# The RWKV-7 scan of a two-layer trunk: five chain outputs kept in PSUM until one copy, one operand for the states of both directions, and long VectorE instructions issued as two halves

## The chip, the cores and the metric

The kernel runs on one core of one Trainium2 chip. The metric is the device time of one execution in microseconds (us). Times of several runs are given by their median. Engines are called by their short names: PE (TensorE matmuls), PEld (the weight loads of PE), DVE (VectorE), ACT (ScalarE), POOL (GpSimd), SP (the queue that issues all DMAs here).

## What is computed

One inference step of a trunk of two layers, for 128 context tokens and 512 latent tokens of width 2048, all in float32. Layer 0 (attention) is not touched by the change. Layer 1 is a bidirectional RWKV-7 mixer with 32 heads of 64; its recurrence, cut to what matters, is:

```python
def wkv7_scan(s0, r, decay, k, v, kk, a, reverse):
    def step(s, inp):
        r_t, w_t, k_t, v_t, kk_t, a_t = inp
        sa = jnp.einsum('bhij,bhj->bhi', s, -kk_t)
        s = s * w_t[:, :, None, :] + sa[..., None] * (kk_t * a_t)[:, :, None, :] + v_t[..., None] * k_t[:, :, None, :]
        return s, jnp.einsum('bhij,bhj->bhi', s, r_t)
...
for z in range(2):                     # two directions, summed
    s_fin, y = wkv7_scan(s_init[z], r, decay[:, :, z], k_z, v, kk, a_z, z == 1)
    ...                                # group norm of y, bonus
y = (outs[0] + outs[1]) * silu(gate)
return y @ w_out
```

Context scans start from zero, latent scans from a given state of their direction; the final context states are outputs too.

## The kernel before, in words

Projections (`project_steps`, L111 to L128) multiply float32 numbers as three products of rounded parts: a weight tile arrives by DMA as `raw`, ACT rounds it to `whi` (L100), POOL subtracts to `wlo` (L101), and PE runs the products into the PSUM tile `pj` (L126), two halves of 320 tokens each. Such a pair of matmuls is the filler of the whole second layer: `fill(w)` (L1482) issues w pairs (`quota[1]` is 1 in the chain) between two pieces of other work.

The tokens (512 latent, 128 context) are ten chunks of 64. The scan goes by channel tile i (16 tiles of 128 channels, two heads each) and u (0 or 1, the two halves of the token axis as the two directions meet them), so 32 units (i, u). `unit(n)` (L1495) writes out PE's order by hand (`manual_schedule`, L1559). It has two parts. In part one the generator `stage_c` (L1284), the chain, advances through five chunk steps s = 0 to 4, and between its yields `P1` steps other stages (the inverse's preparation `stage_a3`, the rates `stage_a1` and group norm `stage_gn` of neighbouring units) and `fill` puts pairs of matmuls (`CW`, 3, 3, 2 and 3 by the yield's number). In part two the list `P2` interleaves the block inverse `stage_inv`, `stage_bk`, `stage_pre`, `stage_bonus` and the Gram products `stage_a2` of the next units with filler. The order on DVE, ACT, POOL and SP is not written by hand: a scheduler places each instruction by priority; `stage_c` and `stage_inv` are wrapped in `urgent` (L1470), which raises theirs. Every engine then works its own list strictly in order.

One chain step does this. PE multiplies the state S by a chunk's operand into C (L1330), DVE makes `rhs` from C and MV (L1337), PE multiplies it by the block inverse `xd` into `pu` (L1349), the two directions' halves of `pu` are copied to UV, one by ACT (L1351) and one by DVE (L1352), PE makes the state's increment `pn` (L1359) and the chunk's output part from UV (L1295, `y_uv`), DVE adds the old state (L1364 or L1374) and multiplies by the decay `dcj` (L1365 or L1376), and that is S of the next step. The output part from the old state is added on PE in the next step (L1303, `y_state`, ahead of L1330), and ACT then copies the output from `Y` to `Yn` (L1307, `y_out`).

All of C, Y, pu, pn and the scratch of the block inverse (PA, PB) lie in one PSUM tile `CC` of two banks. Where two engines touch the same bank, the framework makes the later instruction wait for the earlier one, also where both only read: L1307 waits for L1337, and L1349 waits for L1307.

A direction's state starts fresh (from `state`) or ends inside a tile, so in some steps only one direction has one: in u = 0 direction 1 begins at s = 2, in u = 1 direction 0 ends after s = 2. Then S is a list with None, the matmuls of the missing direction are left out, `rhs` is made for 64 rows by L1337 and for 64 by L1341, and the state is updated per direction (L1374 and L1376) instead of jointly (L1364 and L1365).

On DVE, beside the chain: the recursion of the inverse of 16 by 16 blocks (L1149 to L1166; its input `Lp` comes by DMA, its result goes by DMA to `Xd` and back to `DD`, which L1174 transposes), the k normalisation (L1029), the cumulated rates (L1075, a scan along tokens), operands (L1085 to L1099), the masks of the Gram products (L1120), the bonus (L1429), and the end of a tile (L1438, L1440).

Of the kernel before, what the change touches and what calls it, by code (L numbers as in the profile page):

```python
# [53 lines left out]
def kernel(  # L54
# [785 lines left out]
    with ExitStack() as l1:  # L840
# [24 lines left out]
        for t in xds + [Lpw]:  # L865
            dve.memset(t, 0.0)
# [10 lines left out]
        blkr = b1.tile([128, 128], F32R, name="blkr")  # L877
        act.activation(out=blkr, in_=blkm, func=AF.Copy)
# [141 lines left out]
        def stage_kk(i):  # L1020
# [8 lines left out]
            dve.scalar_tensor_tensor(out=kk, in0=t.kT, scalar=V("k_k", i), in1=kk, op0=ALU.mult, op1=ALU.mult)  # L1029
# [40 lines left out]
        def stage_e(i, u):  # L1070
# [4 lines left out]
            dve.tensor_tensor_scan(out=D, data0=scm, data1=rate, initial=0.0, op0=ALU.mult, op1=ALU.add)  # L1075
# [19 lines left out]
            dve.tensor_scalar(out=az, in0=az, scalar1=V("k_a", i), scalar2=ck1[:, i:i + 1], op0=ALU.mult, op1=ALU.add)  # L1095
# [29 lines left out]
        def stage_a3(i, u):  # L1125
# [35 lines left out]
            dve.tensor_tensor(out=sb[P_], in0=bc8(Xp[P_, lo8, lo8].rearrange("p s j -> p j s"), 1),
                              in1=bc8(Lp[P_, lo8, hi8].rearrange("p s r -> p r s"), 2), op=ALU.mult)
            dve.tensor_reduce(out=W[P_], in_=sb[P_], axis=AX.X, op=ALU.add)
            dve.tensor_tensor(out=sb[P_], in0=bc8(Xp[P_, hi8, hi8], 2),
                              in1=bc8(W[P_].rearrange("p q j -> p j q"), 1), op=ALU.mult)
            dve.tensor_reduce(out=Xp[P_, hi8, lo8], in_=sb[P_], axis=AX.X, op=ALU.add, negate=True)  # L1166
# [117 lines left out]
        def stage_c(i, u):  # L1284
            t, un = tiles_[i], units[(i, u)]
            AR, BKn, UV, xd, GG, dcj = un.AR, un.BKn, un.UV, un.xd, un.GG, un.dcj
            S, joint = carry.get("S"), carry.get("joint")
            Yn = un.Yn = u1.tile([128, 5, 2, 64], F32, tag="yz", name="Yn", bufs=2)
            Y = CC[:, :, 64:128]

            def y_uv(s, S, cgs):
# [5 lines left out]

            def y_state(s, S, cgs):
                for h in range(2):
                    hs = slice(64 * h, 64 * h + 64)  # L1300
                    for z in range(2):
                        if S[z] is not None:
                            pe.matmul(Y[64 * z:64 * z + 64, h, :], AR[hs, cgs[z], 1, :], S[z][hs, :],  # L1303
                                      start=False, stop=True)

            def y_out(s, S, cgs):
                act.activation(out=Yn[:, s], in_=Y, func=AF.Copy)  # L1307

            for s in range(5):
                loc = (s, 4 - s)  # L1310
                cgs = (un.ca[0] + loc[0], un.ca[1] + loc[1])
                if u == 0 and s == 0:
                    st = u1.tile([128, 64], F32, tag="st", name="st", bufs=2)
                    dma(out=st, in_=state[0, i])
                    S, joint = [st, None], None
                if u == 0 and s == 2:
                    st = u1.tile([128, 64], F32, tag="st", name="st", bufs=2)
                    dma(out=st, in_=state[1, i])
                    S, joint = [S[0], st], None
                if u == 1 and s == 3:  # L1320
                    S, joint = [None, S[1]], None
                C = CC[:, :, 0:64]
                pu, pn = (CC[:, 1, 128:256], CC[:, 0, 128:256]), CC[:, 0, 128:256]
                if s:
                    y_state(*ys)
                for h in range(2):
                    hs = slice(64 * h, 64 * h + 64)
                    for z in range(2):
                        if S[z] is not None:
                            pe.matmul(C[64 * z:64 * z + 64, h, :], AR[hs, cgs[z], 0, :], S[z][hs, :],  # L1330
                                      start=True, stop=True)
                rhs = u1.tile([128, 128], F32, tag="rhs", name="rhs")
                mv = un.MV[:, s, :]
                for p, ok in (((0, 128), True),) if None not in S else (((0, 64), S[0]), ((64, 128), S[1])):
                    p = slice(*p)
                    if ok is not None:
                        dve.scalar_tensor_tensor(out=rhs[p].rearrange("p (h d) -> p h d", h=2), in0=C[p],  # L1337
                                                 scalar=-1.0, in1=mv[p].rearrange("p (h d) -> p h d", h=2),
                                                 op0=ALU.mult, op1=ALU.subtract)
                    else:  # L1340
                        dve.tensor_scalar(out=rhs[p], in0=mv[p], scalar1=-1.0, scalar2=None, op0=ALU.mult)  # L1341
                if s:
                    y_out(*ys)
# [8 lines left out]
                dve.tensor_copy(out=UV[64:128, cgs[1], :], in_=pu[1][64:128])  # L1352
# [10 lines left out]
                if joint is not None and all(need):  # L1363
                    dve.tensor_tensor(out=Sn, in0=pn[:, 0:128].rearrange("p (z d) -> p z d", z=2), in1=joint, op=ALU.add)  # L1364
                    dve.tensor_tensor(out=Sn, in0=Sn,  # L1365
                                      in1=dcj[:, s, :].rearrange("p (z o) -> p z o", o=1).to_broadcast([128, 2, 64]),
                                      op=ALU.mult)
                else:
                    for z in range(2):
                        if not need[z]:  # L1370
                            continue
                        pz = pn[:, 64 * z:64 * z + 64]
                        if S[z] is not None:
                            dve.tensor_tensor(out=Sn[:, z, :], in0=pz, in1=S[z], op=ALU.add)  # L1374
                            pz = Sn[:, z, :]
                        dve.tensor_scalar(out=Sn[:, z, :], in0=pz, scalar1=dcj[:, s, z:z + 1], scalar2=None, op0=ALU.mult)  # L1376
# [57 lines left out]
        def stage_end(i, u):  # L1434
# [3 lines left out]
            dve.tensor_scalar(out=t.ysum, in0=t.ysum, scalar1=V("ln_w", i), scalar2=lnb2[:, i:i + 1],  # L1438
# [258 lines left out]
```

## Time and profile before

| What | Value |
|---|---|
| median of 3 runs | 3674.24 us (3662.57, 3674.24, 3682.79) |
| the profiled execution's own time | 3666.42 us |
| its span (first to last instruction) | 3664.6 us |
| mean granted clock of PE | 0.982 |
| busy in the span: PE, DVE, ACT, POOL | 94%, 60%, 44%, 33% |

The profile is of one execution. "Idle before" is the time in which an engine had nothing running ahead of an instruction, and the arrow names what released it. In a timeline row stand start, duration, engine, line, operation, output and inputs, count of merged instructions, and in brackets the idle time and its releaser. Matmuls are pipelined and their ends are modelled, so the idle time of PE is counted from a modelled end; that of PEld is counted from the last weight load, and comes out longer for the same gap.

### The profile page before, as it was taken

The numbers are of one execution on the slowest core, as the hardware profiler recorded it, in microseconds if no ns is written. First come the engines' busy times: TensorE is split into PE (matmuls) and PEld (weight loads), VectorE is DVE, ScalarE is ACT, GpSimd is POOL, SyncE is SP. The second block draws the span as 40 slices with busy tenths as digits, with TensorE's granted clock in tenths as the row PEclk, the third lists the DMA queues.
The fourth block names the chain that finished last, engine by engine and source line by source line (L and its number), as shares of the span: only waits on it lengthen the run. The fifth ranks groups of instructions, "written<-read, shape, count | busy, mean of one in ns | idle before, by whom it ended". The sixth has DMA issues, their size and how long they took to land. (4 is left out here: it accounts for less than half of the span.)

```text
span 3664.6 us, 83198 instructions
## 1 busy us (share of the span) xinstructions
PE 3443.2 (94%) x34176; PEld 3014.7 (82%) x34176; DVE 2190.1 (60%) x4232; ACT 1608.0 (44%) x3310; POOL 1192.0 (33%) x1094
## 2 busy tenths in 40 slices
PE   8999999999999999999999999999999999998998
PEld 4788889988888889888777777778888878777898
DVE  3346655666666674556666666766666666666402
ACT  3344443444444422544454454545454545545322
POOL 1222122222222344432332333323333333333444
PEclk9999999999999999999999999999999999999999
DMA  9623423333333464332222222222222222223534
GB/s 332 221 69 103 125 89 116 108 107 106 108 107 112 149 211 153 105 79 65 68 64 71 59 66 75 65 67 64 65 74 68 62 66 70 67 74 95 159 97 144
DMA packets 388462, 376.18 MB, mean 103 GB/s; under 512 B 200496, under 2 KB 242416, under 8 KB 388080
## 3 DMA queue, kind: packets, MB, share of 16 engines
q1 hardware_dynamic: 388080, 370.86, 34.7%
q8 instruction: 268, 4.39, 0.5%
q14 instruction: 114, 0.93, 0.1%
HBM read 328.51 MB, written 42.24 MB: 101 GB/s over the span
## 5 line engine op out<-in xcount | busy, mean ns | idle before, releaser
L101 POOL TENSOR_TENSOR wlo<-raw,whi 128x512 fp32r<-128x512 f32 (+1 forms) x628 | 859.1, 1369 | 1982.5 <-PE pj L126 1239.1
L126 PE MATMUL pj<-h0hi,wlo 128*128 128x320 f32 x4448 | 1088.2, 324 | 17.2 <-POOL wlo L101 17.2
L126 PE MATMUL pj<-h0hi,whi 128*128 128x320 f32 x4448 | 1087.1, 324 | 4.5 <-DVE gt L953 3.2
L126 PE MATMUL pj<-h0lo,whi 128*128 128x320 f32 x4448 | 1080.7, 322 | 1.1 <-POOL h0lo L101 0.8
L126 PEld LDWEIGHTS pj<-h0hi,wlo 128*128 128x128 f32 x4448 | 747.6, 191 | 51.5 <-POOL wlo L101 20.8
L126 PEld LDWEIGHTS pj<-h0hi,whi 128*128 128x128 f32 x4448 | 746.4, 191 | 37.7 <-issue 8.5
L126 PEld LDWEIGHTS pj<-h0lo,whi 128*128 128x128 f32 x4448 | 749.8, 191 | 29.2 <-issue 8.2
L100 ACT ACTIVATE whi<-raw 128x512 fp32r<-128x512 f32 (+1 forms) x628 | 390.7, 623 | 734.3 <-PE pj L126 430.2
L200 DVE SCALAR_TENSOR_TENSOR aacc<-araw,scs,aacc 128x512 f32<-128x512 f32 x480 | 409.8, 902 | 16.8 <-DMA araw<-in_dram 15.9
L364 DVE TENSOR_REDUCE nm<-S 128x1 f32<-128x768 f32 (+1 forms) x120 | 98.4, 820 | 256.1 <-PE S L376 255.9
L724 DVE SCALAR_TENSOR_TENSOR x<-pj,mod,xr 128x512 f32<-128x512 f32 (+2 forms) x68 | 33.3, 525 | 248.6 <-PE pj L126 243.1
L367 ACT ACTIVATE P<-S,nm 128x768 f32<-128x768 f32 (+1 forms) x120 | 95.1, 792 | 166.1 <-DVE nm L364 165.6
L1120 DVE TENSOR_TENSOR GG<-gram,con 128x512 f32<-128x512 f32 (+1 forms) x192 | 107.8, 596 | 75.4 <-PE gram L1116 75.3
L1116 PE MATMUL gram<-AR,BK 64*128 64x128 f32 x1280 | 120.6, 301 | 26.1 <-DVE GG L1120 14.6
L1307 ACT ACTIVATE Yn<-CC 128x128 f32<-128x128 f32 x160 | 44.3, 277 | 220.7 <-DVE rhs L1337 209.7
L1116 PEld LDWEIGHTS gram<-AR,BK 64*128 64x128 f32 x1280 | 95.7, 196 | 52.3 <-DVE GG L1120 24.2
L1352 DVE COPY UV<-CC 64x128 f32<-64x128 f32 x160 | 47.1, 294 | 130.2 <-ACT UV L1351 128.7
L1056 PE MATMUL plo<-lr,lw 96*128 96x320 f32 x256 | 104.2, 489 | 6.4 <-DMA lr<-lorad 6.2
L1351 ACT ACTIVATE UV<-CC 64x128 f32<-64x128 f32 x160 | 43.0, 269 | 149.4 <-PE CC L1349 148.9
L566 PE MATMUL po<-PT,vt 128*128 128x128 f32 x800 | 103.4, 277 | 0.1
L566 PEld LDWEIGHTS po<-PT,vt 128*128 128x128 f32 x800 | 98.3, 192 | 4.3 <-issue 2.5
L1058 ACT ACTIVATE tmp<-plo,vecs 128x320 f32<-128x320 f32 x128 | 67.4, 527 | 66.8 <-PE plo L1056 66.8
(339 smaller groups left out, 5219.0 us busy)
## 6 DMA issues: line engine op xcount, KB each, us to landing
raw<-in_dram SPq DMA_DIRECT2D x612, 256.0 KB
araw<-in_dram SPq DMA_DIRECT2D x384, 256.0 KB
lr<-lorad SPq DMA_DIRECT2D x128, 120.0 KB
Ld<-GG SPq DMA_DIRECT2D x64, 160.0 KB
lw<-in_dram SPq DMA_DIRECT2D x128, 48.0 KB
x<-in_dram SPq DMA_DIRECT2D x16, 320.0 KB
xr<-in_dram SPq DMA_DIRECT2D x16, 320.0 KB
DD<-Xd SPq DMA_DIRECT2D x32, 160.0 KB
```

The source lines that it names most:

```text
L100: act.activation(out=hi, in_=src, func=AF.Copy)
L101: (lo_eng or pool).tensor_tensor(out=lo, in0=src, in1=rf(hi), op=ALU.subtract)
L126: pe.matmul(p[:n, 0:b - a], w, x[:, kk ^ flip, a:b], start=(kk == order[0] and i == 0), stop=(kk == order[-1] + kc - 1 and i == 2))
L200: dve.scalar_tensor_tensor(out=acc[:, s], in0=raw, scalar=scs[:, k, s:s + 1], in1=acc[:, s], op0=ALU.mult, op1=ALU.add)
L364: dve.tensor_reduce(out=nm, in_=S[:, 0:nk], axis=AX.X, op=ALU.max, negate=True)
L367: act.activation(out=P[:, 0:nk], in_=S[:, 0:nk], func=AF.Exp, bias=nm, accum_out=l)
L566: pe.matmul(po[:, 0:128], H.vt[:, kt, :], PT[:, j, :], start=(j == 0), stop=(j == n - 1))
L1056: pe.matmul(ps[:, 0:HT], lw, lo, start=True, stop=True)
L1058: act.activation(out=hv(tmp, z, ca, cb), in_=c3(ps[:, 0:HT]), func=AF.Exp, scale=-1.0, bias=nw0[:, bcol:bcol + 1])
L1116: pe.matmul(ps[:, j * 128:(j + 1) * 128], BK[hs, c + j, :, :].rearrange("p a t -> p (a t)"), AR[hs, c + j, :, :].rearrange("p a t -> p (a ...
L1120: dve.tensor_tensor(out=GG[:, c:c + n, h, :], in0=ps[:, 0:n * 128].rearrange("p (j t) -> p j t", t=128), in1=maskg.rearrange("p (o t) -> p ...
L1352: dve.tensor_copy(out=UV[64:128, cgs[1], :], in_=pu[1][64:128])
```

## The change

Four things are edited together.

1. **Outputs stay in PSUM through the chain.** `Ys` takes five output slots of 64 columns in each bank of `CC` (columns 192 to 511; `pu` and `pn` move to 64 to 191). `y_uv` and `y_state` write slot s. The five copies L1307 become one copy of 128x640 after the last step (L1376 of the changed kernel), and `Yn` has one buffer instead of two.
2. **The states are one operand.** S is always a tile slice with both directions: `Sn`, or two neighbouring slots of a new tile `ZS` of four slots, of which slot 1 (and, until a state is loaded there, the one in use) is zero. The matmuls of a missing direction now run on zeros, `rhs` is one instruction of 128 rows, the state update is one add and one multiply (for one direction only, or into `ZS`, at the places where a direction starts or ends). Both initial states of a tile are loaded at its first step.
3. **The second copy to UV goes from DVE to ACT.**
4. **Long DVE instructions are issued as two halves:** L1029, L1075, L1095, L1429, L1438 and L1440 (640 columns to twice 320), and L1161, L1163, L1164, L1166 (512 to twice 256).

To make room, the 128 columns `blkm` of the constants are loaded at the beginning of layer 1 into a work buffer instead of at the start of the kernel.

```diff
         Lpw = b1.tile([128, 272], F32, name="Lp")
-        for t in xds + [Lpw]:
+        ZS = b1.tile([128, 4, 64], F32, name="ZS")
+        for t in xds + [Lpw, ZS]:
             dve.memset(t, 0.0)
...
+        blkm = u1.tile([128, T], F32, tag="t0", name="blkm")[:, 0:128]
+        dma(out=blkm, in_=consts[:, 256:384])
         act.activation(out=blkr, in_=blkm, func=AF.Copy)
...
-            dve.tensor_tensor_scan(out=D, data0=scm, data1=rate, initial=0.0, op0=ALU.mult, op1=ALU.add)
+            for a, b in HALVES:
+                dve.tensor_tensor_scan(out=D[:, a:b], data0=scm[:, a:b], data1=rate[:, a:b], initial=0.0,
+                                       op0=ALU.mult, op1=ALU.add)
...
-            dve.tensor_tensor(out=sb[P_], in0=bc8(Xp[P_, hi8, hi8], 2),
-                              in1=bc8(W[P_].rearrange("p q j -> p j q"), 1), op=ALU.mult)
-            dve.tensor_reduce(out=Xp[P_, hi8, lo8], in_=sb[P_], axis=AX.X, op=ALU.add, negate=True)
+            for o in (0, 4):
+                os_ = slice(o, o + 4)
+                dve.tensor_tensor(out=sb[P_, os_], in0=bc8(Xp[P_, 8 + o:12 + o, hi8], 2),
+                                  in1=bc8(W[P_].rearrange("p q j -> p j q"), 1), op=ALU.mult)
+                dve.tensor_reduce(out=Xp[P_, 8 + o:12 + o, lo8], in_=sb[P_, os_], axis=AX.X, op=ALU.add, negate=True)
...
-            Yn = un.Yn = u1.tile([128, 5, 2, 64], F32, tag="yz", name="Yn", bufs=2)
-            Y = CC[:, :, 64:128]
+            Yn = un.Yn = u1.tile([128, 5, 2, 64], F32, tag="yz", name="Yn")
+            Ys = CC[:, :, 192:512].rearrange("p h (s d) -> p s h d", d=64)
...
                     for z in range(2):
-                        if S[z] is not None:
-                            pe.matmul(Y[64 * z:64 * z + 64, h, :], AR[hs, cgs[z], 1, :], S[z][hs, :],
-                                      start=False, stop=True)
-
-            def y_out(s, S, cgs):
-                act.activation(out=Yn[:, s], in_=Y, func=AF.Copy)
+                        pe.matmul(Ys[64 * z:64 * z + 64, s, h, :], AR[hs, cgs[z], 1, :], S[hs, z, :], start=False, stop=True)
...
-                if s:
-                    y_out(*ys)
                 yield 0
...
                 act.activation(out=UV[0:64, cgs[0], :], in_=pu[0][0:64], func=AF.Copy)
-                dve.tensor_copy(out=UV[64:128, cgs[1], :], in_=pu[1][64:128])
+                act.activation(out=UV[64:128, cgs[1], :], in_=pu[1][64:128], func=AF.Copy)
...
+                dve.tensor_tensor(out=Sn[:, kept, :], in0=pn3[:, kept, :], in1=S[:, kept, :], op=ALU.add)
+                ys = (s, S, cgs)
+                if (u, s) in ((0, 1), (1, 2)):
+                    dve.tensor_scalar(out=ZS[:, 2, :], in0=Sn[:, u, :], scalar1=dcj[:, s, u:u + 1], scalar2=None, op0=ALU.mult)
+                    S = ZS[:, 1:3, :] if u else ZS[:, 2:4, :]
...
                 else:
...
+                    dve.tensor_tensor(
+                        out=Sn[:, kept, :], in0=Sn[:, kept, :], in1=dcj[:, s, kept].rearrange(
+                            "p (z o) -> p z o", o=1).to_broadcast([128, sum(need), 64]), op=ALU.mult)
+                    S = Sn
...
             y_state(*ys)
-            y_out(*ys)
+            act.activation(out=Yn, in_=Ys, func=AF.Copy)
             yield 3
...
+            for a, b in HALVES:
+                y = t.ysum[:, a:b]
+                dve.tensor_scalar(out=y, in0=y, scalar1=V("ln_w", i), scalar2=lnb2[:, i:i + 1], op0=ALU.mult, op1=ALU.add)
+                dve.tensor_tensor(out=y, in0=y, in1=t.vT[:, a:b], op=ALU.add)
```

PE's filler stands between the chain's pieces in the same numbers as before. On DVE and ACT the scheduler gives another order. Three places follow; the rows are an engine's list in order, with line, operation, output and inputs, and shape.

DVE in unit (3, 0), from the k normalisation `kk` and the inverse's last products (`sb`, `sw`, `Xp`) to `rhs` of s = 3; before:

```order
L1029 SCALAR_TENSOR_TENSOR kk<-kT,vecs,kk 128x640
L1161 TENSOR_TENSOR sb<-Xp,Lp 104x512
L1352 COPY UV<-CC 64x128
L1163 TENSOR_REDUCE sw<-sb 104x64
L1164 TENSOR_TENSOR sb<-Xp,sw 104x512
L1374 TENSOR_TENSOR S<-CC,S 128x64
L1374 TENSOR_TENSOR S<-CC,st 128x64
L1376 TENSOR_SCALAR S<-S,dcj 128x64 x2
L1166 TENSOR_REDUCE Xp<-sb 104x8x8
L1337 SCALAR_TENSOR_TENSOR rhs<-CC,MV 128x128
```

The same place in the changed kernel:

```order
L1174 TENSOR_TENSOR sb<-Xp,Lp 104x256 x2
L1033 SCALAR_TENSOR_TENSOR kk<-kT,vecs,kk 128x320 x2
L1176 TENSOR_REDUCE sw<-sb 104x32 x2
L1359 TENSOR_TENSOR S<-CC,ZS 128x128
L1179 TENSOR_TENSOR sb<-Xp,sw 104x256
L1368 TENSOR_TENSOR S<-S,dcj 128x128
L1181 TENSOR_REDUCE Xp<-sb 104x4x8
L1179 TENSOR_TENSOR sb<-Xp,sw 104x256
L1412 TENSOR_TENSOR ysum<-ysum,pgn 128x256
L1335 SCALAR_TENSOR_TENSOR rhs<-CC,MV 128x128
L1181 TENSOR_REDUCE Xp<-sb 104x4x8
```

The copy to UV has left this list, the state's add now stands ahead of both halves of the product L1179 and its multiply between them, and the last reduction into `Xp` stands behind `rhs` instead of ahead of it. Three pairs of halves still stand back to back ahead of the add.

DVE in the same unit, from the state's multiply after s = 3 to the end of the tile before (`ysum`); before:

```order
L1365 TENSOR_TENSOR S<-S,dcj 128x128
L1422 TENSOR_TENSOR ysum<-ysum,pgn 128x64
L1438 TENSOR_SCALAR ysum<-ysum,vecs 128x640
L1337 SCALAR_TENSOR_TENSOR rhs<-CC,MV 128x128
L1440 TENSOR_TENSOR ysum<-ysum,vT 128x640
L1352 COPY UV<-CC 64x128
```

The same place in the changed kernel:

```order
L1368 TENSOR_TENSOR S<-S,dcj 128x128
L1412 TENSOR_TENSOR ysum<-ysum,pgn 128x64
L1432 TENSOR_SCALAR ysum<-ysum,vecs 128x320 x2
L1335 SCALAR_TENSOR_TENSOR rhs<-CC,MV 128x128
L1433 TENSOR_TENSOR ysum<-ysum,vT 128x320 x2
```

Both halves of the scaling (L1432) still stand ahead of `rhs` of s = 4.

ACT in the same unit, s = 3 to the end of the chain, among the rates (`tmp`, `rate`, `az`), `whi` of the weights and an evacuation `vT`; before:

```order
L1307 ACTIVATE Yn<-CC 128x128
L1351 ACTIVATE UV<-CC 64x128
L1058 ACTIVATE tmp<-plo,vecs 128x320
L100 ACTIVATE whi<-raw 128x512
L1307 ACTIVATE Yn<-CC 128x128
L1351 ACTIVATE UV<-CC 64x128
L889 ACTIVATE vT<-pj,c_14605 128x640
L1058 ACTIVATE tmp<-plo,vecs 128x5x64
L1062 ACTIVATE tmp<-tmp,epsb 128x640
L1067 ACTIVATE az<-tmp 128x640
L1307 ACTIVATE Yn<-CC 128x128
```

The same place in the changed kernel:

```order
L1345 ACTIVATE UV<-CC 64x128
L1346 ACTIVATE UV<-CC 64x128
L1063 ACTIVATE tmp<-plo,vecs 128x320
L100 ACTIVATE whi<-raw 128x512
L1345 ACTIVATE UV<-CC 64x128
L1346 ACTIVATE UV<-CC 64x128
L892 ACTIVATE vT<-pj,c_14605 128x640
L1063 ACTIVATE tmp<-plo,vecs 128x5x64
L1067 ACTIVATE tmp<-tmp,epsb 128x640
L1072 ACTIVATE az<-tmp 128x640
L1376 ACTIVATE Yn<-CC 128x640
```

The copies of single outputs are gone, the two copies to UV stand next to each other, and the one long copy stands where the last short one stood.

More of the change, by code (lines that the diff above doesn't have):

```diff
@@ L75 @@
     dma(out=vecs, in_=vec[:, 0:NV0])
-    con = cst.tile([128, 384], F32, name="con")
-    dma(out=con, in_=consts)
-    ident, maskg, blkm = (con[:, i:i + 128] for i in range(0, 384, 128))
+    con = cst.tile([128, 256], F32, name="con")
+    dma(out=con, in_=consts[:, 0:256])
+    ident, maskg = (con[:, i:i + 128] for i in range(0, 256, 128))
     ones = cst.tile([128, 128], F32, name="ones")
@@ L1094, in stage_e @@
                 pool.tensor_copy(out=un.dcj[:, :, z], in_=dsrc[:, ::-1] if z else dsrc)
-            dve.tensor_scalar(out=az, in0=az, scalar1=V("k_a", i), scalar2=ck1[:, i:i + 1], op0=ALU.mult, op1=ALU.add)
+            for a, b in HALVES:
+                dve.tensor_scalar(out=az[:, a:b], in0=az[:, a:b], scalar1=V("k_a", i), scalar2=ck1[:, i:i + 1],
+                                  op0=ALU.mult, op1=ALU.add)
             for z, a, b, ca, cb in zh:
@@ L1312, in stage_c @@
                 if u == 0 and s == 0:
[L1313 to L1321, printed above, removed]
+                    dma(out=ZS[:, 0, :], in_=state[0, i])
+                    dma(out=ZS[:, 3, :], in_=state[1, i])
+                    S = ZS[:, 0:2, :]
                 C = CC[:, :, 0:64]
-                pu, pn = (CC[:, 1, 128:256], CC[:, 0, 128:256]), CC[:, 0, 128:256]
+                pu, pn = (CC[:, 1, 64:192], CC[:, 0, 64:192]), CC[:, 0, 64:192]
                 if s:
@@ L1328, in stage_c @@
                     for z in range(2):
-                        if S[z] is not None:
-                            pe.matmul(C[64 * z:64 * z + 64, h, :], AR[hs, cgs[z], 0, :], S[z][hs, :],
-                                      start=True, stop=True)
+                        pe.matmul(C[64 * z:64 * z + 64, h, :], AR[hs, cgs[z], 0, :], S[hs, z, :], start=True, stop=True)
                 rhs = u1.tile([128, 128], F32, tag="rhs", name="rhs")
[L1333 to L1341, printed above, removed]
-                if s:
-                    y_out(*ys)
+                dve.scalar_tensor_tensor(out=rhs.rearrange("p (h d) -> p h d", h=2), in0=C, scalar=-1.0,
+                                         in1=un.MV[:, s, :].rearrange("p (h d) -> p h d", h=2),
+                                         op0=ALU.mult, op1=ALU.subtract)
                 yield 0
@@ L1437, in stage_end @@
             t = tiles_[i]
[L1438 to L1440 removed]
+            for a, b in HALVES:
+                y = t.ysum[:, a:b]
+                dve.tensor_scalar(out=y, in0=y, scalar1=V("ln_w", i), scalar2=lnb2[:, i:i + 1], op0=ALU.mult, op1=ALU.add)
+                dve.tensor_tensor(out=y, in0=y, in1=t.vT[:, a:b], op=ALU.add)
             if i < 15:
```

52 lines of the change are left out of this document (22 added, 30 removed).

## The prediction, made before the changed kernel was run

> **What bounds the kernel now.** The page's head gives the span, and the table of stretches, restricted to the scan, the busy time of PE, PEld, DVE, ACT and POOL, the granted clock, the DMA share and the rate:
>
> ```profile
> span 3664.6 us, 83198 instructions
> 1645.00:3420.00 1775.00, 1657.78 (x22578) 1405.06 (x22575) 1180.27 (x2672) 865.71 (x1920) 576.54 (x636) 0.98 0.28 71
> ```
>
> In the 1775 us of the scan PE is busy for 1658, at a granted clock of 0.98. PE is the bound, and a change that takes no matmul away can gain only from the 117 us in which PE stands. So the next view is that of the waits, over the same stretch: who stood, for whom, microseconds in all, number of cases, the longest.
>
> ```profile
> PE CC L1349 <- ACT Yn L1307: 19.9, 38, 2.4
> PE gram L1116 <- DVE GG L1120: 14.6, 17, 2.7
> PE CC L1359 <- DVE UV L1352: 14.3, 19, 1.1
> PE CC L1303 <- DVE S L1374: 10.4, 24, 1.5
> PE CC L1330 <- DVE S L1376: 7.5, 10, 1.8
> PE CC L1303 <- DVE S L1364: 6.7, 8, 1.3
> PEld CC L1349 <- ACT Yn L1307: 33.8, 58, 2.7
> PEld CC L1359 <- DVE UV L1352: 21.9, 31, 1.3
> PEld CC L1303 <- DVE S L1374: 18.3, 30, 1.8
> ```
>
> All but the Gram line are waits in the chain, and each is met by one of the edits: the copy to Yn, the copy to UV on DVE, the state's add and multiply. PE's accounting gives 58.8 us for the five (19.9 + 14.3 + 10.4 + 7.5 + 6.7); that of the weight loads, which counts the same gaps from another end, gives 74.0 against 44.6 for the three that both show, 1.66 times as much. The timeline then says why they come about. First a `rhs` that came late:
>
> ```profile
> 2008.60 1.29 POOL L101 TENSOR_TENSOR wlo<-raw,whi 128x512 fp32r<-128x512 f32 x1
> 2008.62 1.67 DVE L1438 TENSOR_SCALAR ysum<-ysum,vecs 128x640 f32<-128x640 f32 x1
> 2010.22 0.27 DVE L1337 SCALAR_TENSOR_TENSOR rhs<-CC,MV 128x128 f32<-128x128 f32 x1
> 2010.53 0.28 ACT L1307 ACTIVATE Yn<-CC 128x128 f32<-128x128 f32 x1 [2.74 <-DVE rhs L1337]
> 2010.85 0.45 PE L1349 MATMUL CC<-rhs,xd 64*64 64x64 f32 x8 [0.80 <-ACT Yn L1307]
> ```
>
> A long instruction stands in front of `rhs` on DVE; then, because of the shared bank, the copy to Yn waits for `rhs`, and L1349 for the copy. Second, a copy to UV and a state's add that came late:
>
> ```profile
> 1998.05 1.74 DVE L1029 SCALAR_TENSOR_TENSOR kk<-kT,vecs,kk 128x640 f32<-128x640 f32 x1
> 1999.70 1.02 DVE L1161 TENSOR_TENSOR sb<-Xp,Lp 104x512 f32<-104x512 f32 x1
> 2000.76 0.29 DVE L1352 COPY UV<-CC 64x128 f32<-64x128 f32 x1
> 2001.11 0.45 PE L1359 MATMUL CC<-UV,BKn 128*64 128x64 f32 x8 [1.09 <-DVE UV L1352]
> 2001.81 1.15 DVE L1164 TENSOR_TENSOR sb<-Xp,sw 104x512 f32<-104x512 f32 x1
> 2002.98 0.23 DVE L1374 TENSOR_TENSOR S<-CC,S 128x64 f32<-128x64 f32 x1
> 2003.40 0.27 PE L1303 MATMUL CC<-S,AR 64*64 64x64 f32 x1 [0.43 <-DVE S L1374]
> ```
>
> The bound of this stage is thus PE with the length of DVE's list in front of three short urgent instructions.
>
> **The change part by part.** The sum is made against the profiled execution, 3666.42 us, which is its span and 1.8 us around it.
>
> *A. No copy between `rhs` and L1349.* `rhs` ends at 2010.49 and L1349 starts at 2010.85; at the 0.04 us that stand between `rhs` and the copy it could start at 2010.53, so the hop is 0.32 us. Over PE's 38 cases that is 12.2 us, over the weight loads' 58 cases 18.6. The `rhs` behind L1438 keeps the rest of its wait, 0.48 of 0.80, since both halves of L1438 stand back to back ahead of it in the new order. I take −15, between the two.
>
> *B and C. UV without DVE, one add and one multiply, halves.* I work through the second piece above with the new order of DVE. L1161 and L1029 as two halves each, at 0.08 more per split (below), end at 1998.05 + 1.02 + 1.74 + 0.16 = 2000.97. The two reductions L1163 come next; in the old run L1163 fits between 2001.05 and 2001.81, so 0.76 at most, 0.84 split. The add starts at about 2001.81 instead of 2002.98, since L1164 now stands behind it and UV is long there. That is 1.17 us earlier, of PE waits of 1.09 + 0.43 = 1.52: 77%. Applied to PE's four lines (14.3 + 10.4 + 7.5 + 6.7 = 38.9) this is 30. I take a little less, since pieces behind L1438 do not move: −12 for B, that is most of the copy's 14.3 to 21.9 less what returns at the add, and −16 for C.
>
> *Price of the halves.* The order shows 256 more instructions on DVE from splits and 160 copies fewer. The nearest rows for a split are two instructions of 320 columns and one of 640, each with two operands in SBUF (the group rows give minimum, median and maximum in ns, first and last start):
>
> ```profile
> 2025.74 0.89 DVE L1085 TENSOR_TENSOR BK<-kk,az 128x320 f32<-128x320 f32 x2 [0.32 <-PE pbk L1184]
> L1440 DVE TENSOR_TENSOR ysum<-ysum,vT x16: 807/809/824, 1781.5 to 3442.2; 128x640 f32<-128x640 f32 x16
> L1438 DVE TENSOR_SCALAR ysum<-ysum,vecs x16: 611/1494/1677, 1779.9 to 3441.5; 128x640 f32<-128x640 f32 x16
> L1120 DVE TENSOR_TENSOR GG<-gram,con 128x512 f32<-128x512 f32 x120 | 78.2, 685 | 37.1 <-PE gram L1116 37.0
> L1120 DVE TENSOR_TENSOR GG<-gram,con 128x256 f32<-128x256 f32 x62 | 23.7, 420 | 28.4 <-PE gram L1116 28.4
> ```
>
> The first two give 0.89 − 0.81 = 0.08 us per split; the last two, which read PSUM, 2 × 0.420 − 0.685 = 0.155. I take 0.08, as nearly all halves work in SBUF: 256 × 0.08 = 20.5 us, against 160 × 0.29 = 46 us of copies that leave. DVE as a whole gets lighter by some 26 us. In part one this lies under PE's filler. In part two PE already waits for the masks L1120 (17 cases, 14.6 us), 80 of the splits stand there and no copy leaves: 6.4 us of DVE work, about half of it in front of a mask that PE waits for: +3.5, bounds 0 and 80 × 0.155 = 12.4. [...]
>
> L1438 takes 1.67 us in the piece beside a POOL instruction of 1.29, and 0.61 at its fastest. [...]
>
> *Matmuls on zeros.* PE gets 256 more. The price of a missing direction is seen where L1330 runs with eight matmuls and with four:
>
> ```profile
> 2052.60 0.34 PE L1330 MATMUL CC<-S,AR 64*64 64x64 f32 x8
> 2052.88 0.56 PE L126 MATMUL pj<-h0hi,whi 128*128 128x320 f32 x2
> ...
> 2059.06 0.33 PE L1330 MATMUL CC<-S,AR 64*64 64x64 f32 x4 [0.81 <-DVE S L1376]
> 2059.32 0.56 PE L126 MATMUL pj<-h0hi,wlo 128*128 128x320 f32 x2
> ```
>
> From start to the next start 0.28 against 0.26, so 0.02 for four, 0.005 each: 256 × 0.005 = 1.3 us (bounds 0 and, if each took an eighth of 0.28, 9).
>
> *The one long copy.* It ends the unit, and L1245, in the same bank, waits for it:
>
> ```profile
> 2014.72 0.28 ACT L1307 ACTIVATE Yn<-CC 128x128 f32<-128x128 f32 x1 [0.38 <-DVE S L1365]
> 2015.66 0.51 PE L1245 MATMUL CC<-DD,GG 32*32 32x16 f32 x39
> L889 ACT ACTIVATE vT<-pj,c x16: 776/776/795, 1595.5 to 3244.2; 128x640 f32<-128x640 f32 x16
> ```
>
> The short copy ends at 2015.00, 0.66 us ahead of L1245. A copy of 640 columns from PSUM takes 0.776 on ACT, 0.50 more, and 0.16 us are left, filled by PE's filler. So I cost it at nothing. If ACT reaches the copy later than now by d, it costs 32 × (d − 0.16): 11 us for d = 0.5. ACT itself gets 160 second copies to UV at 0.28 (45 us) and 32 × 0.78 = 25 us of long copies for 160 × 0.28 = 45 us of short ones, some 25 us more on an engine that is busy for less than half of the stretch.
>
> *DMA.* `DD` comes by a round trip through `Xd`. Where it is late, DVE stands at L1174 (idle 17.0 us in 14 cases) with the urgent add behind it:
>
> ```profile
> 1953.61 0.51 DVE L1174 STREAM_TRANSPOSE DD<-DD 128x320 f32<-128x320 f32 x1 [3.35 <-DMA DD<-Xd]
> 1954.43 0.40 PE L1303 MATMUL CC<-S,AR 64*64 64x64 f32 x8 [1.53 <-DVE S L1374]
> ...
> DVE DD L1174: 17.0, 14
> ```
>
> There DVE stood 3.35 us and PE 1.53. The last reduction into `Xp` now stands behind `rhs`, so the trip starts a little later: +2, about one more such case. The load of `blkm` at the start of layer 1 is waited for once, between 0 and the 3.35 of this row: +1. Both initial states are loaded at a tile's first step instead of one later: nothing, SP issues as many transfers as before and in the old places but for that one.
>
> The sum: −15 − 12 − 16 + 3.5 + 1.3 + 2 + 1 = −35, to 3631 on the profiled execution. That execution is 7.8 us below the median of the runs; the median comes to 3674.24 − 35 = 3639.
>
> **The rivals.** *1, no change.* The halves buy nothing since the scheduler sets them back to back, as the order shows for L1029, L1161, L1163 and L1438, and what the copy to UV gives free returns in full at the add, which stands behind the same work. Then only A is left with all the costs: −15 + 8 = −7, 3667. For it: each pair back to back. Against it: L1164 is really moved behind the add, 1.15 us in the piece above. Chance 0.16. *2, slower.* In the odd units DVE meets the transpose L1174 ahead of the state's add, and the trip of `DD` starts later, behind `rhs`; each us by which `DD` is later is a us for which DVE stands with the chain behind it. The row above has it once: PE lost 1.53. To come out slower by over 0.5% it must eat the 35 and 18 more, so 53 / 16 = 3.3 us of PE in every odd unit, and the time is 3693. Against it: only 14 of 32 transposes waited, 17.0 us in all, so the trip would have to be late by more than twice the worst. Chance 0.06. *3, twice the gain.* The weight loads' accounting is the true one: the terms A to C grow 1.66 times, 43 to 71, and with the same costs −63, 3611. For it: the matmul ends are modelled, and PE may stand for longer than its row says. Against: 71 of the 117 us of PE's idle time would have to go. Chance 0.10.
>
> **How the numbers follow.** The forecast, 3639, has 0.68; its own range is 3620 to 3655, from the bounds of the unknown costs (A between 12.2 and 18.6, part two up to 12.4, zeros up to 9, the long copy up to 11) and the 28 of B and C taken between 20 and 39. The runs of the kernel before lie within 0.3% of their median, so a change under 0.5%, 18.4 us, can hardly be told from none. Faster than 3655.9: the forecast and rival 3, 0.78. Within: rival 1, 0.16. Slower: 0.06. The range of 8 in 10 reaches from beyond rival 3, 3606, to the lower part of rival 1, 3664, and leaves out rival 2, the rest of rival 1 and a little below.
>
> **What would show it.** Right: in the waits, no line of L1353 (before L1359) behind DVE; the line of L1343 now behind `rhs` with under 10 us by PE's count; the lines for the state's add and multiply together under 12. PE's idle time in the scan falls from 117 to about 80, its busy time grows by 1 to 3. Halves: two of 320 columns at 0.08 more than one of 640. L1260 starts as soon after the filler as L1245 did. Wrong: a new line of PE at L1260 behind the long copy of over 5 us; waits for L1174 of over 30 us on DVE; PE's busy time in the scan higher by over 10 us, which would mean that zeros cost; or the lines of the state's add as long as the copy's line is now.

## The result, and the profile after

| | before | changed |
|---|---|---|
| median, 6 runs each | 3665.94 us (3662.57 to 3682.79) | 3636.07 us (3633.18 to 3648.30) |
| ratio, 95% interval | 1 | 0.9917 [0.9903, 0.9931] |
| profiled execution, mean granted clock | 3666.42 us, 0.982 | 3634.34 us, 0.988 |

The change saves 30 us; forecast were 35, with 3639 for the time. The total came out, but more than half of it by a term that was not in the sum. The page's head and the table of stretches, the changed kernel:

```profile
span 3632.5 us, 84033 instructions
1645.00:3420.00 1775.00, 1670.12 (x23106) 1419.45 (x23101) 1143.28 (x2702) 902.87 (x1977) 588.29 (x647) 0.99 0.29 74
```

PE's count of busy time in a fixed stretch says little here, since the changed kernel gets further in it. So I take the same work in both: from the first to the last matmul of the inverse's first piece (L1245 before, L1260 now), 32 units. Before, then changed:

```profile
1623.60:3365.90 1742.30, 1628.91 (x22353) 1380.16 (x22352) 1156.94 (x2631) 841.73 (x1858) 562.73 (x627) 0.98 0.27 68
```

```profile
1631.80:3337.90 1706.10, 1607.21 (x22600) 1362.30 (x22600) 1107.18 (x2640) 865.42 (x1889) 557.97 (x626) 0.99 0.27 70
```

The stretch is 36.2 us shorter. PE stood for 113.4 us (1742.30 − 1628.91) and now stands for 98.9: 14.5 less. But PE is also busy for 21.7 us less, with 247 matmuls more. The granted clock explains it. Read in windows of 1 us, it is 1.00 nearly everywhere and falls to 0.50 for 3.4 us at a time, in some places for two or three such times in a row; each 3.4 us at 0.50 cost 1.7 us. Before has 13 places with drops in the stretch, 34.1 us in all; the changed kernel 7, 11.9 us. Without them PE is busy for 1594.8 us before and 1595.3 now. So of 36 us, 14.5 are waits and 22 are clock.

PE's waits in the same stretch of the trace as in the prediction (1645 to 3420, as in all lists of waits below), changed kernel:

```profile
PE CC L1282 <- ACT xd L1276: 25.6, 26, 2.8
PE CC L1317 <- DVE S L1359: 15.4, 30, 1.3
PE gram L1125 <- DVE GG L1129: 13.2, 21, 1.3
PE CC L1333 <- DVE S L1368: 9.6, 22, 1.1
PE CC L1343 <- DVE rhs L1335: 8.8, 13, 1.1
PE CC L1269 <- DVE t L1263: 7.5, 12, 0.7
...
PE gram L1125 <- ACT MV L1237: 3.4, 6, 1.3
...
PE CC L1269 <- issue: 2.4, 5, 0.9
...
PE CC L1260 <- DMA DD<-Xd: 1.5, 1, 1.5
```

and rows of before that the prediction did not show:

```profile
PE CC L1267 <- ACT xd L1261: 14.6, 16, 2.6
...
PE gram L1116 <- ACT MV L1222: 8.4, 19, 1.1
...
PE CC L1330 <- DVE S L1365: 2.7, 6, 0.5
...
PE CC L1254 <- issue: 1.4, 3, 0.6
```

The wait behind Yn has become one behind `rhs`, 8.8 instead of 19.9. The one for UV on DVE is gone (14.3). The state's add and multiply, 10.4 + 7.5 + 6.7 + 2.7 = 27.3 before, are still 25.0. And the block inverse waits more: L1282 and L1269 together 35.5 where L1267 and L1254 had 16.0.

The two pieces that the prediction worked through, in the changed kernel. First `rhs` behind the scaling of `ysum`:

```profile
2008.42 1.28 POOL L101 TENSOR_TENSOR wlo<-raw,whi 128x512 fp32r<-128x512 f32 x1 [8.35 <-DMA Xd<-Xp]
2008.50 1.97 DVE L1432 TENSOR_SCALAR ysum<-ysum,vecs 128x320 f32<-128x320 f32 x2
...
2010.40 0.28 DVE L1335 SCALAR_TENSOR_TENSOR rhs<-CC,MV 128x128 f32<-128x128 f32 x1
...
2010.73 0.45 PE L1343 MATMUL CC<-rhs,xd 64*64 64x64 f32 x8 [0.69 <-DVE rhs L1335]
```

The hop over ACT is gone, but the two halves take 1.97 us beside POOL's instruction where the whole took 1.67, so the wait is 0.69 instead of 0.80 and not the 0.48 that I had left it. One half alone, minimum, median and maximum in ns:

```profile
L1432 DVE TENSOR_SCALAR ysum<-ysum,vecs x32: 427/434/1624, 1784.6 to 3409.9; 128x320 f32<-128x320 f32 x32
```

A half can take 1.62 us, nearly as long as the whole. POOL's instruction ends at 2009.70, and the slow first half ends 0.42 us later, about the time that an undisturbed half takes (0.43). Of the 16 first halves, the nine that start within 0.1 us behind POOL's `wlo` take 1.37 to 1.62 us, and the seven with less than 0.2 us of POOL's work beside them 0.43 to 0.44. Then UV and the add:

```profile
1999.25 0.27 ACT L1345 ACTIVATE UV<-CC 64x128 f32<-64x128 f32 x1 [0.32 <-DVE Xp L1164]
1999.26 1.79 DVE L1174 TENSOR_TENSOR sb<-Xp,Lp 104x256 f32<-104x256 f32 x2
1999.53 0.27 ACT L1346 ACTIVATE UV<-CC 64x128 f32<-64x128 f32 x1
...
2000.76 0.45 PE L1353 MATMUL CC<-UV,BKn 128*64 128x64 f32 x8
2000.98 1.00 DVE L1033 SCALAR_TENSOR_TENSOR kk<-kT,vecs,kk 128x320 f32<-128x320 f32 x2
...
2001.91 0.73 DVE L1176 TENSOR_REDUCE sw<-sb 104x32 f32<-104x256 f32 x2
...
2002.56 0.27 DVE L1359 TENSOR_TENSOR S<-CC,ZS 128x128 f32<-128x128 f32 x1
...
2002.89 0.34 PE L1317 MATMUL CC<-ZS,AR 64*64 64x64 f32 x8 [0.27 <-DVE S L1359]
...
2003.62 0.34 PE L1333 MATMUL CC<-S,AR 64*64 64x64 f32 x8 [0.39 <-DVE S L1368]
```

UV is ready at 1999.80 and nobody waits for it. The add stands behind three pairs of halves; of 1.09 + 0.43 of PE waits, 0.27 + 0.39 are left.

### The profile page after: what moved, and what is told of

The parts are those of the page before. It is cut to its first block, busy times and chain, and to the rows that moved or that the text cites. A ratio compares the mean times of both kernels' runs of the same rounds, so it can differ in the third digit from the quotient of the medians.

```text
span 3632.5 us, 84033 instructions
## 1 busy us (share of the span) xinstructions
PE 3426.5 (94%) x34432; PEld 2997.9 (83%) x34432; DVE 2141.9 (59%) x4249; ACT 1632.0 (45%) x3342; POOL 1190.0 (33%) x1094
## 5 line engine op out<-in xcount | busy, mean ns | idle before, releaser
L200 DVE SCALAR_TENSOR_TENSOR aacc<-araw,scs,aacc 128x512 f32<-128x512 f32 x480 | 409.5, 901 | 16.6 <-DMA araw<-in_dram 15.8
L1359 DVE TENSOR_TENSOR S<-CC,S 128x128 f32<-128x128 f32 (+1 forms) x112 | 29.9, 267 | 118.8 <-PE CC L1310 78.6
L1335 DVE SCALAR_TENSOR_TENSOR rhs<-CC,MV 128x128 f32<-128x128 f32 x160 | 45.8, 286 | 69.9 <-PE CC L1333 69.6
L1343 PEld LDWEIGHTS CC<-rhs,xd 64*64 64x64 f32 x1280 | 49.8, 133 | 42.8 <-DVE rhs L1335 20.8
```

Source lines behind the costliest of these rows:

```text
L200: dve.scalar_tensor_tensor(out=acc[:, s], in0=raw, scalar=scs[:, k, s:s + 1], in1=acc[:, s], op0=ALU.mult, op1=ALU.add)
L1335: dve.scalar_tensor_tensor(out=rhs.rearrange("p (h d) -> p h d", h=2), in0=C, scalar=-1.0, in1=un.MV[:, s, :].rearrange("p (h d) -> p h d" ...
L1343: pe.matmul(pu[z][o:o + 64, hs], xd[o:o + 64, 2 * loc[z] + h, :], rhs[o:o + 64, hs], start=True, stop=True)
```

## The experiments

Theory W was the prediction's: the time follows PE's waits. After the first four runs it was replaced by theory K: time = busy at full clock + PE's waits + clock drops, where a drop follows a gap of PE of more than about 1.2 us (the counts stand in the last section). The table collects the runs; 7 is a single execution and stands in its own paragraph. "Lost, runs" is one less the mean granted clock, times the span, averaged over all runs of that kernel; "waits", "lost" and "drops" are those of the profiled execution between the first and the last matmul of the inverse's first piece; the last column is PE's busy time there less "lost".

| kernel | time to before [95%] | clock, mean | lost, runs | waits | lost (drops) | busy at full clock |
|---|---|---|---|---|---|---|
| before (29 runs beside the first four) | 1 | 0.9826 | 64.0 | 113.4 | 34.1 (13) | 1594.8 |
| changed | 0.9917 [0.9903, 0.9931] | 0.9877 | 44.9 | 98.9 | 11.9 (7) | 1595.3 |
| 1 no halves | 1.0008 [0.9993, 1.0022] | 0.9765 | 86.3 | 97.6 | 46.0 (19) | 1594.7 |
| 2 halves in the chain's part alone | 0.9909 [0.9887, 0.9931] | 0.9833 | 60.7 | 88.0 | 27.5 (13) | 1594.3 |
| 3 Yn copied per step | 0.9989 [0.9974, 1.0004] | 0.9835 | 60.5 | 114.5 | 29.4 (13) | 1593.6 |
| 4 UV half on DVE | 0.9962 [0.9948, 0.9977] | 0.9856 | 52.7 | 109.3 | 15.4 (7) | 1596.1 |
| 5 no joint state | 0.9962 [0.9947, 0.9977] | 0.9836 | 59.9 | 108.3 | 21.5 (11) | 1591.0 |
| 6 before with halves | 1.0044 [1.0028, 1.0059] | 0.9815 | 68.2 | 119.4 | 25.7 (11) | 1597.3 |
| 8 no halves, filler moved | 0.9933 [0.9912, 0.9955] | 0.9818 | 66.2 | 94.4 | 22.9 (12) | 1591.3 |
| 9 changed, filler moved | 0.9853 [0.9832, 0.9874] | 0.9875 | 45.3 | 91.0 | 10.2 (5) | 1589.2 |
| 10 as 2, filler moved | 0.9861 [0.9842, 0.9880] | 0.9870 | 47.1 | 91.9 | 12.2 (7) | 1592.8 |
| 11 as 10, and in part two | 0.9851 [0.9832, 0.9870] | 0.9872 | 46.2 | 89.6 | 13.6 (8) | 1592.0 |
| 12 add delayed | 0.9995 [0.9982, 1.0008] | 0.9832 | 61.8 | 114.8 | 13.6 (7) | 1597.6 |

Times in microseconds of experiments 1 to 4 stand beside 3674.7 us for before, of 5 to 8 beside 3673.3, of 9 to 12 beside 3675.9. The changed kernel's stand beside only 3665.94, of six runs, and it was not run beside the later ones. Its distance to an experiment is thus uncertain by up to 0.27%: experiment 1 lies 33 us above it by the ratios and 38 in microseconds, and the table's parts add up to 39.5 (−1.3 of waits, −0.6 of busy time, 41.4 of clock). The expectations are in microseconds, and a hit or miss of less than some 10 us tells little.

**1. No halves.** All ten instructions whole again, for instance:

```diff
-            for a, b in HALVES:
-                dve.tensor_tensor_scan(out=D[:, a:b], data0=scm[:, a:b], data1=rate[:, a:b], initial=0.0,
-                                       op0=ALU.mult, op1=ALU.add)
+            dve.tensor_tensor_scan(out=D, data0=scm, data1=rate, initial=0.0, op0=ALU.mult, op1=ALU.add)
```

> The changed kernel with the ten long DVE instructions whole again (edit 4 undone, the rest kept). In the trace of the changed kernel two halves cost far more than my 0.08 us: over 30 units the scan went from 44.5 to 58.5 us, the rates' scaling from 19.3 to 29.5, the bonus from 14.4 to 23.7, and PE's waits in the block inverse behind them grew by about 20 us. Theory W (the gain is the chain's waits; halves give perhaps 8 us at the state's add and cost 10 to 15 in part two): 3631 us beside 3636 for the changed kernel, with the inverse's PE waits back at about 20. Rival H (short DVE instructions carry the gain): 3650 or more. Rival S (the joint operand saves PE time and the granted clock is higher; halves do nothing): 3636.

Measured: 3674.35 us, 1.0008, the whole gain gone. Theory W's 3631 is refuted in the time and right in the waits: 97.6 against 98.9. The time is in rival H's range, but not by the waits. What differs is the clock: 0.9765 on average, no run above 0.979, the changed kernel none below 0.985. PE's waits of this kernel for the state's add and multiply, and for the inverse:

```profile
PE CC L1317 <- DVE S L1359: 23.1, 34, 1.5
PE CC L1333 <- DVE S L1368: 13.1, 22, 1.3
PE CC L1282 <- ACT xd L1276: 13.0, 16, 1.9
...
PE CC L1333 <- DVE ZS L1362: 6.0, 8, 1.5
```

Add and multiply have 42.2 us (23.1 + 13.1 + 6.0) where the changed kernel has 25.0, the inverse some 20 less. The halves move waits from the chain to the inverse; at the add and the multiply they cut the longest from 1.5 to 1.3 us, at the inverse it grew from 1.9 to 2.8. What a long one does is seen here, the table of stretches (length, PE, PEld, DVE, ACT, POOL, then the granted clock) and the timeline of the same place:

```profile
2788.00:2792.00 4.00, 3.24 (x32) 2.57 (x31) 3.90 (x6) 2.67 (x6) 0.40 (x1) 1.00 0.35 109
2792.00:2794.00 2.00, 0.84 (x17) 0.64 (x18) 2.00 (x6) 0.00 (x0) 0.00 (x0) 0.97 0.00 0
2794.00:2796.00 2.00, 2.00 (x14) 1.67 (x13) 0.31 (x2) 0.00 (x0) 0.00 (x0) 0.50 0.51 57
```

```profile
2790.79 0.45 PE L126 MATMUL pj<-h0hi,wlo 128*128 128x320 f32 x2
...
2792.72 0.35 PE L1317 MATMUL CC<-ZS,AR 64*64 64x64 f32 x8 [1.47 <-DVE S L1359]
...
2793.51 0.34 PE L1333 MATMUL CC<-S,AR 64*64 64x64 f32 x8 [0.44 <-DVE S L1368]
2793.78 0.83 PE L126 MATMUL pj<-h0hi,whi 128*128 128x320 f32 x2
```

PE stands 1.47 us for the add and 0.44 for the multiply, and the pair of matmuls behind it takes 0.83 us instead of 0.45, at half the clock. Of this kernel's 19 drops, 11 have the state's add or multiply as the longest wait in the 4.5 us ahead of them; of the changed kernel's 7, three.

**2. Halves in the chain's part alone** (k normalisation and the recursion's products; scan, rates' scaling, bonus and the tile's end whole, as in experiment 1).

> The changed kernel with only the k normalisation and the recursion's four products in halves; scan, rates' scaling, bonus and the end of the tile whole. Theory W: part two gets its time back and the state's add keeps what it won: 3625 us, DVE busy in the scan about 30 us less than in the changed kernel. Rival H: 3645, since half of the halves are gone. Rival S: 3636.

Measured: 3641.29 us, 0.9909, the same as the changed kernel's 0.9917. The waits fell, as theory W said, from 98.9 to 88.0; the clock took it back, 60.7 lost instead of 44.9. DVE's busy time in the scan fell by 11 us (1143.28 to 1132.26), not by 30.

**3. The output copied after each step.**

```diff
-            Ys = CC[:, :, 192:512].rearrange("p h (s d) -> p s h d", d=64)
+            Y = CC[:, :, 64:128]
...
+                if s: act.activation(out=Yn[:, s - 1], in_=Y, func=AF.Copy)
```

> The changed kernel with the output copied to Yn after each step again (edit 1 undone: one slot Y, two buffers of Yn). Theory W: the hop between rhs and the product with the inverse comes back on 35 to 58 cases of 0.32 us: +15, 3651 us. Rival S: 3636, the hop was hidden by the filler and its wait only changes its name.

Measured: 3666.32 us, 0.9989. PE's waits have the hop again:

```profile
PE CC L1344 <- ACT Yn L1338: 22.9, 44, 1.4
```

The waits grow by 15.6 us (114.5 against 98.9), the 15 of the prediction; the loss by 15.6 in the mean of the runs. The rival, a mere change of name, is refuted.

**4. The second copy to UV on DVE.**

```diff
-                act.activation(out=UV[64:128, cgs[1], :], in_=pu[1][64:128], func=AF.Copy)
+                dve.tensor_copy(out=UV[64:128, cgs[1], :], in_=pu[1][64:128])
```

> The changed kernel with the second copy to UV on DVE again (edit 3 undone). Theory W: PE waits for that copy again, +12 us, 3648 us. Rival R (the copy's wait had only moved to the state's add behind the same DVE list, so that undoing it moves it back): 3636 within 5.

Measured: 3657.86 us, 0.9962. Waits:

```profile
PE CC L1353 <- DVE UV L1346: 17.4, 20, 1.3
...
PE CC L1317 <- DVE S L1359: 8.6, 19, 1.3
```

17.4 us come at the copy and the add has 6.8 less than in the changed kernel: both theory and rival R hold a part. The stretch has 10.4 us more of waits, against the 12 expected, and the runs lost 7.8 us more to the clock.

**5. Without the joint state operand** (the kernel before with edits 1, 3 and 4).

> The kernel before with edits 1, 3 and 4 but without the joint state operand (edit 2 left out). Theory K, formed from the first four runs: the time is a part at full clock (busy matmuls and PE's idle time; 3610 us before, 3594 in the changed kernel) and a part lost to the granted clock (one less the mean clock, times the span; 64 us before, 45 in the changed kernel), and a drop of the clock follows a gap of PE of over about 1.2 us. By it the state's update per direction brings back some 10 us of waits and some 8 us of lost clock: 3655. Rival S: if the joint operand gives nothing, 3636. If the joint operand is what saves, 3665.

Measured: 3658.35 us, 0.9962, near the 3655 of theory K. The reason given for it did not show: the state's adds and multiplies wait 17.0 us (8.6, 4.4, 3.7 and 0.3 by line), less than the 25.0 of the changed kernel. The 9.4 us more of waits are spread, 5 of them in one DMA wait at the scan's end; the loss is 15 us more, not 8. Which gaps of the update per direction cause it was not found: no drop of the trace stands behind the state's add or multiply.

**6. Halves alone, on the kernel before.**

> The kernel before with edit 4 alone. Theory K: the chain's waits get 8 us shorter and part two's 12 longer, 3613 us at full clock; the longest gaps get shorter, so 50 lost instead of 64: 3663. Rival H (halves carry the gain by themselves): 3640. If neither: 3675.

Measured: 3688.27 us, 1.0044: slower than before by 15 us, outside of all three expectations. Waits rise by 6 us, with the hop at Yn at 29.1 instead of 19.9 and the inverse's third piece at 23.3 instead of 14.6; the loss is 4 us more. Rival H is refuted: halves by themselves gain nothing. Where the 15 us come from is not shown: in the traced execution the stretch is as long as before (1742.4 us), and 14 us lie ahead of it (it starts at 1637.6 instead of 1623.6), 6.8 of them lost clock, in a part that the edit hardly touches.

**7. Experiment 1 once more**, a single execution.

> The changed kernel with all long instructions whole, once more, one look beside the next two: 3674 with about 86 us lost to the clock, 12 or more of the drops within 4 us behind a wait for the state's add (theory K).

Measured: 3663.72 us, clock 0.979, 77 us lost, 96.7 of waits and 24 drops, 16 of them with the state's add or multiply as the longest wait ahead.

**8. No halves, filler moved to the add.**

```diff
-        CW = (3, 3, 2, 3)
+        CW = (3, 2, 3, 3)
```

> The changed kernel with whole instructions, and one pair of filler matmuls per step moved from behind the copies to UV to behind the state's add (3, 2, 3, 3 instead of 3, 3, 2, 3). It shortens the gaps at the add and leaves the halves out. Theory K: 15 us less of waits (3575 at full clock) and about 30 us less lost clock (56): 3631. Rival H (it is the halves as such): 3670 or more, as with the old filler.

Measured: 3647.14 us, 0.9933. Rival H's 3670 is refuted: with whole instructions, a pair of matmuls in the gap at the add gives most of what the halves gave. Drops fell from 19 to 12, four of them at the state's update instead of 11. It stays short of theory K's 3631: the loss only fell to 66 instead of 56, and the waits by 3.2 us (97.6 to 94.4) instead of 15. The add and the multiply have 29.1 us instead of 42.2 (10.8, 14.3 and 4.0), but 4.8 came at the copies to UV and the rest elsewhere. So the gain is mostly clock, 20 us.

**9. The changed kernel with the filler moved** (the same edit).

> The changed kernel, halves and all, with the filler 3, 2, 3, 3. Theory K: the waits for the state's add and multiply (21 us) fall to about 10, some 4 come at the copies to UV; 3586 us at full clock and 40 lost: 3626. Rival: the add's waits were not what cost any more, 3636.

Measured: 3622.51 us, 0.9853, faster than the changed kernel by 0.6% in the ratios and by 13.6 us, 0.4%, in microseconds. Its waits:

```profile
PE CC L1343 <- DVE rhs L1335: 16.4, 26, 0.9
...
PE CC L1317 <- DVE S L1359: 8.0, 14, 0.9
...
PE CC L1333 <- DVE S L1368: 4.7, 16, 0.4
```

Add and multiply went from 25.0 to 12.7; 7.6 of it returned at `rhs`, not at UV as expected. Five drops are left, none at the state's update. In the runs the loss stayed (45.3 beside 44.9), so what is gained are waits (7.9 us) and busy time (6.1), and not clock, of which theory K expected 5.

**10 and 11. Halves in the chain's part, filler moved; and filler moved in part two as well.**

> Halves in the k normalisation and the recursion only, filler 3, 2, 3, 3. Theory K: 3574 us at full clock, 55 lost (the large gaps at the inverse and the Gram products remain): 3629, faster than the same with the old filler (3641).

```diff
-('bk', 1), ('pre', 2), ('inv', 2), ('bonus', 1), ('bk', 1)
+('bk', 1), ('pre', 3), ('inv', 2), ('bonus', 0), ('bk', 1)
```

> As the run before, and one unit of filler moved in part two from behind the first bonus step to ahead of the third piece of the block inverse, where the largest gaps of PE (1.7 to 2.7 us) stand. Theory K: those gaps shrink by about half a us each, 10 us less of waits and 3 drops of the clock fewer: 3615. Rival: the bonus or the fourth piece waits instead, 3629.

Measured: 3629.94 us (0.9861) and 3623.01 (0.9851). Run 10 has theory K's 3629, with 47 lost instead of 55. With the filler at the add, 10 is as fast as 9 within the intervals, so part two's halves give nothing that these runs could show. In 11 the waits of the inverse's fourth and third piece are

```profile
PE CC L1291 <- ACT xd L1287: 19.2, 25, 1.8
...
PE CC L1282 <- ACT xd L1276: 5.9, 8, 1.3
```

where 10 has 7.4 and 17.0: the wait moved on by one piece, which was the rival's case. The waits in all fell by 2.3 us instead of 10, the drops did not get fewer (8 beside 7), and the intervals do not tell 11 from 10.

**12. The add of one step delayed**, by issuing it four times, in the odd units.

```diff
+                for _ in range(4 if (u, s) == (1, 1) else 1):
                     dve.tensor_tensor(out=Sn[:, kept, :], in0=pn3[:, kept, :], in1=S[:, kept, :], op=ALU.add)
```

> The changed kernel with the state's add of s = 1 in the odd units issued four times instead of once, which delays it by about 1.5 us in 16 units (0.29 each, and pieces of the recursion that now slip between). Theory K: 16 gaps of about 1.2 us, so 16 to 20 us more at full clock, and behind more than half of them a drop of the clock of 1.7 us: 20 to 30 us more lost; 3676 in all. Rival L (the clock has nothing to do with the gaps): the same 16 to 20 and the loss as before (45): 3655.

Measured: 3674.15 us, 0.9995; the waits grow by 15.9 us and the loss by 16.9 in the mean of twelve runs (61.8 against 44.9). The time is 38 us above the changed kernel's in microseconds and 29 by the ratios, where theory K had 40 and rival L 19. The time alone thus decides little; it is the loss, which rival L had unchanged, that speaks for theory K. The line of the add:

```profile
PE CC L1317 <- DVE S L1360: 32.1, 41, 3.0
```

The traced execution has the best clock of the twelve (0.986), and in it only two of the seven drops stand behind the add; so the average shows the loss, and this trace does not show its places.

## Why the prediction came out, point by point

- **A, −15.** PE's line went from 19.9 to 8.8, −11.1, short in part by the L1432 pairs: nine of the 16 have a slow first half (1.37 to 1.62 us), and the nine waits behind them are 5.8 of the 8.8. Before, nine of the 16 L1438 were slow (1.49 us and more). Undone alone (3), the waits grow by 15.6. The term stood.
- **B, −12.** The line is gone (−14.3), and undone alone (4) it costs 10.4 us of waits. The term stood.
- **C, −16: failed.** The lines went from 27.3 to 25.0. The step that failed is "77%. Applied to PE's four lines": the piece was worked out as if A and B left the add where it was. They bring `rhs` and UV early, so the add is due early, behind the same list on DVE: with whole instructions the lines stand at 42.2 (1), and the halves take off 17, about my 16, from that. The first rival's "returns in full at the add" was right for 15 us (42.2 against 27.3).
- **Price of the halves, +3.5: mis-sized.** I took 0.08 us per split from L1085 and L1440. Groups of 30 units, before and changed (busy us, mean ns):

```profile
L1075 DVE TENSOR_TENSOR_SCAN D<-scm,rate 128x640 f32<-128x640 bf16 x30 | 44.5, 1484 | 3.5 <-ACT az L1067 3.4
L1095 DVE TENSOR_SCALAR az<-az,vecs,ck 128x640 f32<-128x640 f32 x30 | 19.3, 642 | 0.0
L1429 DVE SCALAR_TENSOR_TENSOR kzs<-rT,vecs,kzs 128x640 f32<-128x640 f32 x15 | 14.4, 957 | 0.0
```

```profile
L1081 DVE TENSOR_TENSOR_SCAN D<-scm,rate 128x320 f32<-128x320 bf16 x60 | 58.5, 999 | 4.4 <-ACT az L1072 4.4
L1103 DVE TENSOR_SCALAR az<-az,vecs,ck 128x320 f32<-128x320 f32 x60 | 29.5, 532 | 0.0
L1420 DVE SCALAR_TENSOR_TENSOR kzs<-rT,vecs,kzs 128x320 f32<-128x320 f32 x30 | 23.7, 824 | 3.5 <-POOL kzs L1112 3.3
```

  33.5 us for 75 splits, 0.45 each. PE's waits at the inverse grew by 19.5, those at the Gram products fell by 6.4 (from 23.0 to 16.6): +13 in place of +3.5. With the halves undone (1) the inverse has 19.9 us less and the Gram products 1.9 more, so the halves' own price is some 18. No run tried why, but the traces show where. With no POOL instruction beside them, the two halves of the scan take 1.63 us where the whole took 1.48 (4 cases each); with one beside them, 2.04 where the whole took 1.49 (28 each). For the rates' scaling it is 0.79 against 0.60, and 1.28 against 0.79. So even undisturbed these splits cost 0.14 and 0.19, and beside POOL about 0.5. My 0.08 came from L1440, which never met a POOL instruction in either trace.
- **Zeros, +1.3.** 247 matmuls more, and busy time at full clock grew by 0.5: as said, nothing to see.
- **The long copy, 0.** No wait of PE for it stands in the list: right by PE's count. The weight loads of L1260 wait for it 5.8 us in 30 cases, 0.19 each.
- **DMA, +3.** DVE stood for `DD` 39.8 us instead of 17.0, above the 30 that I named as wrong. PE lost little by it: 1.5 us at L1260 (1.0 at L1245 before), and 2.0 in three waits for an add behind such a stand (1.5 in one before). `blkm` was waited for, but by ACT:

```profile
1529.05 0.31 ACT L881 ACTIVATE blkr<-blkm 128x128 fp32r<-128x128 f32 x1 [3.04 <-DMA blkm<-in_dram]
```

  PE's only wait beside it is 0.36 us for `wlo`. The stretch starts 8.2 us later than before; 5.1 of it is clock lost ahead of the scan (25.6 against 20.5), the rest stays open.
- **The term that was missing: the clock, −19 in the runs (the changed kernel's six beside 29 later ones of before), −22 in the traces.** My sum took PE's busy time for fixed. The net of the waits, −14.5, is less than half of the −35; the clock made up for it. That the total came out near the forecast is thus partly luck. The four edits hold each other up: undone one by one they cost 0.9, 0.7, 0.45 and 0.45%, 2.5% together, of a gain of 0.8%. The likely reason, that each alone leaves some gap long, is not shown for 4 and 5.
- **The signs that I named.** Seen: no line of L1353 behind DVE, and `rhs` under 10 us. Not seen: add and multiply under 12 us (25.0), and PE's idle time in the fixed stretch near 80 (1775 − 1670.12 = 104.9). PE's busy time in the fixed stretch is 12.3 us up, my sign for costly zeros; but there the changed kernel does more of the work, and over the same work it is 0.5 at full clock.

## What to carry to other kernels

When PE is the bound, look at how long its gaps are as well as at their sum: a gap that dropped the clock cost at least 1.7 us over its own length (3.4 us at 0.50), and a drop came behind 102 of 169 waits with over 1.5 us of idle time in the 3.4 us up to their end, but behind 47 of 1878 with under 1.2, so many short gaps were cheaper here than a few long ones, and a piece of ready work moved into the longest gap (experiment 8) gave most of what finer instructions gave. Compare kernels by PE's busy time at full clock, its waits and its clock apart. Halves are not free: those of part two gave nothing (9 at 0.9853 beside 10 at 0.9861), and on the kernel before all of them together gave nothing (6, at 1.0044). That they pay only where an urgent instruction can be put between them fits this, but was not tried by itself.

## What the runs showed of the hardware

- The granted clock fell from 1.00 to 0.50 for 3.4 us at a time (in the trace of before also for 6.8 and 10.2 us), and did so more often the longer PE had stood. Over the 14 traces, with PE's idle time summed over the 3.4 us up to the end of each wait in the scan: under 1.2 us, a drop began within 4 us behind the wait in 47 of 1878 cases; from 1.2 to 1.5 us, in 59 of 184; above 1.5 us, in 102 of 169. So 1.2 us or more of idle time within 3.4 us was followed by a drop in 161 of 353 cases; what sets its length and its depth was not shown.
- That a gap drops the clock only sometimes fits the spread between runs: the changed kernel's six runs go from 3633.18 us at a clock of 0.990 to 3648.30 at 0.985.
- Over 14 kernels PE's busy time in the scan, less the drops, is 1589 to 1598 us, while its length goes from 1690 to 1742.
